# A hybrid attention, retention and ConvFFN layer on one core: loads of the merge in the order of use, a ring of its own for gate weights, and down-weight sums moved into the retention

## The chip, the core and the metric

The kernel runs on 1 core of one Trainium2 chip. The metric is device time in microseconds (us), the median of three runs. Matrix work runs on TensorE (PE; PEld is its weight load), elementwise work on VectorE (DVE), ScalarE (ACT) and GpSimd (POOL). All large transfers are issued from one queue, that of SyncE (SP). An instruction of an engine, and an issue of SP, starts only when the one before it on that engine has started or ended, so one that waits holds up whatever stands behind it.

## The reference, cut to what matters

One layer over 1024 latent tokens of width 1024 and 256 context tokens:

```python
hx = _modulate(_rmsnorm(x, norm1_g[l]), sh1, sc1)
(xq, xk, xv, xrq, xrk, xrv, xrg, xga, xgb) = jnp.split(hx @ w_in[l], IN_OFFSETS, axis=-1)
o_na = _na_latent(...)                 # 8 heads, neighbourhood attention plus context keys
o_ret = _ret_output(o_ret_x, xrg)      # 4 heads, both directions; normalized, times silu(xrg)
merged = sigmoid(xga) * (o_na @ w_proj_na) + sigmoid(xgb) * (o_ret @ w_proj_ret)
x = x + g1 * (merged @ w_out[l])
hx2 = _modulate(_rmsnorm(x, norm2_g[l]), sh2, sc2)
x = x + g2 * _conv_ffn(hx2, w_up[l], conv_w[l], conv_b[l], w_down[l])
return _rmsnorm(x, final_norm_g)
```

Everything is float32. Each operand of a large product is split into a high part (rounded to the type fp32r) and the remainder, and a product is made of three matmuls: high by high, high by low, low by high.

## The kernel before

The kernel is one Python function that writes out the layer stage by stage; a tile framework puts the instructions of a stage on the five queues, chooses their order within an engine from the dependences, and gives each tile a slot in a ring (`tag`, `bufs`). A tile waits until the slot's previous user is done. The stages, by time in the profile:

- Start and neighbourhood attention, up to 394 us. Filler work in it computes part of the gates ("spilled" ones, stored to DRAM as `d_gate`).
- Retention, 394 to 728 us: 4 heads (class `Head`), each over 2 context chunks and 8 latent chunks, so 40 steps, each called by `slot`. In a step `front` multiplies a chunk by the head's eight weight blocks, POOL adds the two parts of the rotation (tile `r`, L1115) and subtracts for `SS` (L1165), and `state` and the `mix` of the head before follow.
- NA projection, 728 to 788 us (L1313 to L1338): eight transposes groups `tpn` of the attention output read from DRAM, then for each of 8 blocks `db` two chains of 12 matmuls, `pn`. In between `hx_sums` builds eight sums of the input halves, `hxT`, on POOL, DVE and ACT.
- Gates, 795 to 953 us: 8 units (class `Gates`), each a Strassen-like scheme of 7 products (`Seven.step`) in place of 8; each product is 4 blocks by 3 matmuls. So 8 x 7 x 12 = 672 matmuls of 128x128 by 512. A unit loads four weight blocks `wr` (`Seven.load`) and POOL makes four sums of them. Units 0 to 3 produce the retention's output (stored as `d_orr`), units 4 to 7 the remaining merge gates.
- In the same stage, `down_sums` (11 rounds of 4, one every fifth product) loads four blocks `pj` of the down weights, subtracts on POOL (L1422, 44 in all) and stores them as `d_w`, for use at the end of the kernel.
- Merge, 953 to 1084 us: 16 blocks `orr` of the retention output are loaded and split, 32 blocks `sg` of gates and projections are loaded, the row vector `gate1` is loaded, and then for each of 8 `db` the two weight blocks of `w_pret` are loaded and split and two chains of 24 matmuls, `pr`, run: 384 matmuls.
- Output projection, 1084 to 1184 us (`out_proj`, products `om`; `w_out` is multiplied by `gate1` on POOL as it is loaded, L100), then the norm, the up products and convolution to 1640 us, and the down products to the end.

Weights pass through the helper `wload`: a load into the ring `raw` (3 tiles, L90), a copy on ACT to the high part (L86), a subtraction on DVE to the low part (L87), into a tile `wc` of a ring of 6. `orr` is loaded through the same three `raw` tiles.

Of the kernel before, what the change touches and what calls it, by code (L numbers as in the profile page):

```python
# [40 lines left out]
def tile_hybrid_layer(ctx, tc: tile.TileContext, io, dbg=None):  # L41
# [55 lines left out]
    def wload(src, lo_eng=None, mul=None, into=None):  # L97
        raw = rawload(src)
        if mul is not None:
            pool.tensor_tensor(raw, raw, mul, ALU.mult)  # L100
        wc = into if into is not None else wtile()
        split(wc[:, 0], wc[:, 1], raw, lo_eng)
        return wc
# [1121 lines left out]

    def slot(main, mix, head=None, i=None):
# [15 lines left out]
        if head:  # L1242
            head.state(i)
        if mix:
            mix.n += 1
# [30 lines left out]
    for _ in tl:  # L1276
        pass
# [5 lines left out]
    hcpool.release()  # L1283
    tg = sb("hx_sums", "right")
# [4 lines left out]
    NH = NF // 2  # L1289

    def g_ps(name):
        return pg.tile([P, 512], F32, tag="g", bufs=6, name=name)

# [5 lines left out]
    def hx_sums(k):  # L1299
        b = {}  # L1300
        for i, half in ((0, 1), (0, 0), (1, 1), (1, 0)):
            kb, c0 = k + KH * i, half * 512
            b[i, half] = t = onap.tile([P, 512], F32, tag="b", bufs=8, name="b")
# [9 lines left out]
    for n in range(KB):  # L1313
        raw = rawload(d_onat[n * P : (n + 1) * P])
# [6 lines left out]
    hs = None  # L1321
    for db in range(KB):
        wp = [wload(io["w_pna"][db, 0])]
        hs = hs if db % 2 else hx_sums(db // 2)
        for half in range(2):
            sl_ = slice(half * 512, half * 512 + 512)
            m = g_ps("pn")
            mm_a(m, wp, lambda k: ona[0][:, k, sl_], lambda k: ona[1][:, k, sl_])
            t = onap.tile([P, 512], F32, tag="pn", bufs=3, name="pn")
            if (db, 0) in spilled:  # L1330
                g = onap.tile([P, 512], F32, tag="sg", bufs=2, name="sgt")
                sync.dma_start(g, d_gate[2 * db, half])
                act.activation(g, g, AF.Sigmoid)
                vec.tensor_tensor(t, m, g, ALU.mult)
            else:
                act.copy(t, m)
            sync.dma_start(d_pn[db, half], t)
        next(hs)  # L1338
    pool.tensor_tensor(col[:, 16:48], col[:, 16:48], bcol[:, 16:48], ALU.add)  # L1339
    a2 = cpool.tile([P, KB], F32, name="a2")  # L1340
    pool.tensor_scalar(a2, col[:, 32:40], 1.0, None, ALU.add)
    pool.tensor_tensor(a2, a2, gcol[:, 1], ALU.mult)
    tpa = g_ps("tpa")
    pe.transpose(tpa[:32, :P], col[:, 16:48], ident)
    arow = ap_.tile([32, P], F32, name="arow")
    act.copy(arow, tpa[:32, :P])
    sync.dma_start(d_ada, arow)
    ap_.release()
    onap.release()


# [6 lines left out]
    class Seven:  # L1358
        def load(self):
            self.a21, self.a22, self.a11, self.a12 = [self.raw(self.src[b, i]) for b, i in ((1, 0), (1, 1), (0, 0), (0, 1))]  # L1360
# [16 lines left out]
        def step(self, n):  # L1377
            if n == 0:
                self.load()
# [28 lines left out]

    gr = sb("gates", "right")

    def down_sums():
        todo = []
        for j in range(NH):
            ts = []
            for i in range(2):
                for dh in range(2):
                    ts.append(gr.tile([P, 512], F32, tag="pj", bufs=8, name="pj"))
                    sync.dma_start(ts[-1], io["w_down"][dh, NH * i + j])
            while todo:
                sync.dma_start(*todo.pop())  # L1420
            for c, x, y, o in ((1, 1, 0, 0), (3, 3, 1, 1), (2, 3, 0, 3), (4, 2, 3, 2)):
                pool.tensor_tensor(ts[o], ts[x], ts[y], ALU.subtract)  # L1422
                todo.append((d_w[j, c - 1], ts[o]))
            yield
# [569 lines left out]
```

## Time and profile before

| what | us |
|---|---|
| median of 3 runs (1844.21 to 1849.22) | 1846.59 |
| the profiled execution | 1843.57 |
| its span, first to last instruction | 1841.4 |
| PE busy in the span | 1736.1 (94%) |
| DVE, ACT, POOL busy | 1314.1, 852.6, 604.0 |
| longest single idle time of PE | 42.6 |

The profile comes from one execution. A row of the waits names the engine that waited, what it wanted to do, and the instruction or transfer that ended the wait. A row of the timeline gives the start, the duration, and in brackets the idle time just ahead and its releaser. A table of windows gives the busy time of each engine in a stretch, and PEclk, the granted TensorE clock: 1.00 is 2.4 GHz, 0.50 is 1.2 GHz.

### The profile page before, as it was taken

The numbers are of one execution on the slowest core, as the hardware profiler recorded it, in microseconds if no ns is written. First come the engines' busy times: TensorE is split into PE (matmuls) and PEld (weight loads), VectorE is DVE, ScalarE is ACT, GpSimd is POOL, SyncE is SP. The second block draws the span as 40 slices with busy tenths as digits, with TensorE's granted clock in tenths as the row PEclk, the third lists the DMA queues.
The fourth block names the chain that finished last, engine by engine and source line by source line (L and its number), as shares of the span: only waits on it lengthen the run. The fifth ranks groups of instructions, "written<-read, shape, count | busy, mean of one in ns | idle before, by whom it ended". The sixth has DMA issues, their size and how long they took to land.

```text
span 1841.4 us, 24786 instructions
## 1 busy us (share of the span) xinstructions
PE 1736.1 (94%) x8381; PEld 1436.4 (78%) x8381; DVE 1314.1 (71%) x2450; ACT 852.6 (46%) x1841; POOL 604.0 (33%) x493
## 2 busy tenths in 40 slices
PE   8799999999999998989973999999999999999997
PEld 4588888888888887767853878878888888888886
DVE  5977887765676765767852465787999899885756
ACT  5666666653344443533332233454444444554444
POOL 2600000001323224277820350035555455311434
PEclk9899999999999999989996999999999999999999
DMA  9143334321010212568977243452332323486744
GB/s 350 48 120 127 103 123 136 111 83 41 18 58 18 58 58 79 167 233 304 342 243 248 58 131 137 176 199 86 115 115 89 111 86 115 147 292 192 238 154 173
DMA packets 139551, 261.61 MB, mean 142 GB/s; under 512 B 15872, under 2 KB 28320, under 8 KB 139424
## 3 DMA queue, kind: packets, MB, share of 16 engines
q1 hardware_dynamic: 139424, 260.03, 42.1%
q8 instruction: 66, 1.08, 0.3%
q14 instruction: 61, 0.50, 0.1%
HBM read 187.87 MB, written 69.48 MB: 140 GB/s over the span
## 4 chain that ended last, share of the span: by engine, by line
PE 71%; DVE 9%; issue 7%; DMA 6%; POOL 4%; ACT 3%; SPq 1%; POOLq 0%; ACTq 0%; DVEq 0%
PE u L1356 24%; PE y L1356 4%; PE mm L112 3%; PE mm L113 3%; PE mm L114 3%; PE mm L124 3%; PE mm L125 3%; PE mm L123 3%; PE R L511 2%; DVE wc L87 2%; PE ptp L493 2%; PE pr L112 1%; PE pr L113 1%; PE pr L114 1%; PE om L123 1%
## 5 line engine op out<-in xcount | busy, mean ns | idle before, releaser
L1356 PE MATMUL u<-T,wc 128*128 128x512 f32 x960 | 227.2, 392 | 4.1 <-ACT pu L1383 4.1
L1356 PEld LDWEIGHTS u<-T,wc 128*128 128x128 f32 x960 | 180.6, 189 | 45.2 <-ACT pu L1383 7.6
L1356 PE MATMUL y<-wc,ahl 128*128 128x512 f32 x924 | 210.6, 389 | 2.6 <-DVE wc L87 1.8
L1356 PEld LDWEIGHTS y<-wc,ahl 128*128 128x128 f32 x924 | 173.3, 188 | 39.6 <-DVE wc L87 2.5
L87 DVE TENSOR_TENSOR wc<-ur,wc 128x512 fp32r<-128x512 f32 x137 | 124.5, 911 | 65.4 <-ACT wc L86 65.4
L86 ACT CAST wc<-ur 128x512 fp32r<-128x512 f32 x137 | 85.1, 622 | 129.9 <-PE y L1356 72.3
L113 PE MATMUL mm<-low,wc 128*128 128x512 f32 (+1 forms) x328 | 124.0, 378 | 0.0
L1356 PE MATMUL u<-h2a,wc 128*128 128x512 f32 x480 | 112.4, 389 | 0.7 <-DVE pu L1391 0.7
L112 PE MATMUL mm<-hx,wc 128*128 128x512 f32 x264 | 107.2, 406 | 0.3 <-DVE vc L221 0.3
L1356 PEld LDWEIGHTS u<-h2a,wc 128*128 128x128 f32 x480 | 89.9, 188 | 19.9 <-DVE pu L1391 1.1
L114 PE MATMUL mm<-hx,wc 128*128 128x512 f32 x264 | 105.1, 398 | 0.0
L87 DVE TENSOR_TENSOR wc<-wr,wc 128x512 fp32r<-128x512 f32 x56 | 69.9, 1255 | 36.0 <-ACT wc L86 35.6
L1339 POOL TENSOR_TENSOR col<-col,bcol 128x32 f32<-128x32 f32 x1 | 0.3, 253 | 281.9 <-DVE aw L538 281.9
L1356 PE MATMUL u<-hxT,wc 128*128 128x512 f32 x384 | 90.4, 391 | 2.4 <-DVE pu L1391 2.4
L86 ACT CAST wc<-s 128x512 fp32r<-128x512 f32 x80 | 49.6, 622 | 91.9 <-PE u L1356 87.0
L125 PE MATMUL mm<-wc,low 128*128 128x512 f32 (+1 forms) x240 | 91.2, 380 | 0.0
L112 PE MATMUL pr<-orr,wc 128*128 128x512 f32 x128 | 50.7, 396 | 42.6 <-ACT wc L86 42.6
L87 DVE TENSOR_TENSOR wc<-raw,wc 128x512 fp32r<-128x512 f32 x92 | 70.5, 775 | 24.1 <-ACT wc L86 23.8
L87 DVE TENSOR_TENSOR wc<-s,wc 128x512 fp32r<-128x512 f32 x80 | 85.2, 1067 | 2.9 <-ACT wc L86 2.5
L1356 PEld LDWEIGHTS u<-hxT,wc 128*128 128x128 f32 x384 | 72.5, 189 | 17.9 <-issue 2.8
L86 ACT CAST wc<-raw 128x512 fp32r<-128x512 f32 x92 | 57.1, 622 | 43.6 <-DMA raw<-in_w_pret 16.1
L1362 POOL TENSOR_TENSOR s<-ur 128x512 f32<-128x512 f32 x20 | 36.9, 1844 | 121.0 <-DVE wc L87 70.5
(392 smaller groups left out, 4807.6 us busy)
## 6 DMA issues: line engine op xcount, KB each, us to landing
ur<-in_w_up SPq DMA_DIRECT2D x80, 256.0 KB, 2.8
ur<-d_a SPq DMA_DIRECT2D x77, 256.0 KB, 3.1
aw<-in_w_ada SPq DMA_DIRECT2D x32, 512.0 KB, 3.3
pj<-in_w_down SPq DMA_DIRECT2D x44, 256.0 KB, 5.2
d_w<-pj SPq DMA_DIRECT2D x44, 256.0 KB, 4.7
d_a<-sa SPq DMA_DIRECT2D x44, 256.0 KB, 2.0
ur<-d_w SPq DMA_DIRECT2D x44, 256.0 KB, 3.3
d_a<-at SPq DMA_DIRECT2D x33, 256.0 KB, 2.7
```

What stands on the lines that cost most here:

```text
L86: act.copy(hi, src)
L87: (lo_eng or vec).tensor_tensor(lo, src, hi.bitcast(F32), ALU.subtract)
L112: pe.matmul(out, wh, xh, start=k == 0, stop=False)
L113: pe.matmul(out, wh, xl, start=False, stop=False)
L114: pe.matmul(out, wl, xh, start=False, stop=k == n - 1)
L123: pe.matmul(out, ah, bh, start=first, stop=False)
L124: pe.matmul(out, ah, bl, start=False, stop=False)
L125: pe.matmul(out, al, bh, start=False, stop=last)
L493: pe.transpose(tp[:, c], self.Pm[h][:, c * P : (c + 1) * P], ident)
L511: pe.matmul(R[:, h], self.pair.V[:, g, h].rearrange("p a b -> p (a b)"), self.PT[h][:, c].rearrange("p a b -> p (a b)"), start=c == 0, sto ...
L1356: pe.matmul(out, a, b, start=first and n == 0, stop=last and n == 2, skip_group_check=True)
L1362: pool.tensor_tensor(self.s1, self.a21, self.a22, ALU.add)
```

## The change

Six edits:

1. `down_sums` is called from `slot` in the retention: two subtractions after each context step, one after each latent step, what is left after the last head. Its ring `pj` moves to the retention's pool. The subtractions keep their order on POOL.
2. A pool of its own (`rr`, ring `r` of 10 tiles) replaces three rings: it holds the attention output to be transposed, the tiles `b` of `hx_sums`, and the `wr` weights of the gates. It is allocated ahead of the NA projection and released after the gates. The transposed blocks no longer pass through `raw`.
3. The first gate unit's `load` is called at the end of the NA projection, not in the unit's first step.
4. In the merge, the loads come in the order of use: the first `w_pret` blocks, then for half 0 eight `orr` blocks and one `db` of `sg`, then the same for half 1, and from there one `db` of `sg` per step.
5. `w_out` is no longer multiplied by `gate1` on POOL (16 instructions); instead `out_proj` multiplies each product by `gate1` on DVE and then adds `x` (16 instructions more on DVE).
6. The classes stand ahead of the NA projection in the code.

```diff
+    def down_sums():
+        def load(j):
+            ts = [rt.tile([P, 512], F32, tag="pj", bufs=8, name="pj") for _ in range(4)]
+            for t, (i, dh) in zip(ts, ((0, 0), (0, 1), (1, 0), (1, 1))):
+                sync.dma_start(t, io["w_down"][dh, NH * i + j])
+            return ts
+
+        todo, nxt = [], load(0)
+        for j in range(NH):
+            ts, nxt = nxt, load(j + 1) if j + 1 < NH else None
+            for c, x, y, o in ((1, 1, 0, 0), (3, 3, 1, 1), (2, 3, 0, 3), (4, 2, 3, 2)):
+                late(pool.tensor_tensor(ts[o], ts[x], ts[y], ALU.subtract))
+                while todo:
+                    sync.dma_start(*todo.pop())
+                todo.append((d_w[j, c - 1], ts[o]))
+                yield
+        sync.dma_start(*todo.pop())
...
         if head:
             head.state(i)
+            for _ in range(2 if i < NCB else 1):
+                next(down_sums, None)
...
+    rr = sb("gate_raws", "right")
...
+    def g_raw(name):
+        return rr.tile([P, 512], F32, tag="r", bufs=10, name=name)
...
-            b[i, half] = t = onap.tile([P, 512], F32, tag="b", bufs=8, name="b")
+            b[i, half] = t = g_raw("b")
...
-        raw = rawload(d_onat[n * P : (n + 1) * P])
+        raw = g_raw("onr")
+        sync.dma_start(raw, d_onat[n * P : (n + 1) * P])
...
             if n == 0:
-                self.load()
+                if not self.loaded:
+                    self.load()
...
-            t = gr.tile([P, 512], F32, tag="r", bufs=10, name="wr")
+            t = g_raw("wr")
...
         next(hs)
+    gu[0].load()
...
-        if n % 5 == 2:
-            next(down_sums, None)
...
-    for half in range(2):
-        for db in range(KB):
-            split(*orr[half, db], rawload(d_orr[db, :, half * 512 : half * 512 + 512]))
     sg = {}
-    for db in range(KB):
+
+    def merge_load(db):
         for half in range(2):
             sg[db, 0, half] = gtile(half, F32, "sg")
             sync.dma_start(sg[db, 0, half], d_pn[db, half])
...
+    def orr_load(half):
+        for k in range(2 * RH):
+            split(*orr[half, k], rawload(d_orr[k, :, half * 512 : half * 512 + 512]))
...
         wp = [wload(io["w_pret"][db, i]) for i in range(2)]
+        if db + 1 < KB and db:
+            merge_load(db + 1)
         for half in range(2):
+            if db == 0:
+                orr_load(half)
+                merge_load(half)
             m = g_ps("pr")
             mm_a(m, wp, lambda k: orr[half, k][0], lambda k: orr[half, k][1])
...
-        wo[kb, 0] = wload(io["w_out"][0, kb], mul=gate1[:, 0:512], into=t)
+        wo[kb, 0] = wload(io["w_out"][0, kb], into=t)
...
-            vec.tensor_tensor(x1[:, cs], m, x1[:, cs], ALU.add)
+            vec.tensor_tensor(xr[:, cs], m, gate1[:, cs], ALU.mult)
+            vec.tensor_tensor(x1[:, cs], xr[:, cs], x1[:, cs], ALU.add)
```

What this does to the queues, in the words of the two programs (a row is one instruction or a run of equal ones; `out<-in`):

On SP before, at the end of the merge's loads, ahead of the first `pr` product (the 16 `orr` loads and 30 more `sg` loads stand ahead of these rows):

```order
L1502 DMA sg<-d_pn 128x512
L1504 DMA sg<-d_gate 128x512
L1511 DMA gate_10432<-d_ada 128x1024
L91 DMA raw<-in_w_pret 128x512 x16
L91 DMA raw<-in_w_out 128x512 x16
```

The weights of the products come after all loads of `orr` and `sg`.

On SP after, from the last gate units' stores on (`d_gate<-c` is the last one):

```order
L1451 DMA d_gate<-c 128x512
L1509 DMA sg<-d_pn 128x512
L1511 DMA sg<-d_gate 128x512
L1509 DMA sg<-d_pn 128x512
L91 DMA raw<-d_orr 128x512
L1451 DMA d_pn<-c 128x512
L91 DMA raw<-d_orr 128x512 x2
L1511 DMA sg<-d_gate 128x512
L1523 DMA gate_10300<-d_ada 128x1024
L91 DMA raw<-d_orr 128x512 x6
L1509 DMA sg<-d_pn 128x512
L91 DMA raw<-d_orr 128x512 x3
```

The two `w_pret` blocks of the first `db` and the first three `orr` blocks stand further up, among the gates. Thirteen `orr` loads are left behind the gates, with six `sg` loads and `gate1` between them, and `w_pret` for the second `db` follows them.

On SP before, between the NA projection and the gates:

```order
L1337 DMA d_pn<-pn 128x512 x10
L1347 DMA d_ada<-arow 32x128
L1442 DMA wr<-in_w_rg 128x512 x4
L1418 DMA pj<-in_w_down 128x512 x4
L1470 DMA o<-d_oret 128x512
L1442 DMA wr<-in_w_rg 128x512 x4
```

and after:

```order
L1421 DMA wr<-in_w_rg 128x512
L1471 DMA d_pn<-pnt 128x512
L1421 DMA wr<-in_w_rg 128x512 x3
L1471 DMA d_pn<-pnt 128x512 x4
L1421 DMA wr<-in_w_rg 128x512
L1471 DMA d_pn<-pnt 128x512 x2
L1482 DMA d_ada<-arow 32x128
L1421 DMA wr<-in_w_rg 128x512
```

The loads of the first two units moved up among the projection's stores.

On POOL in two steps of the retention, before:

```order
L1165 TENSOR_TENSOR SS<-run,SS 128x256
L1192 TENSOR_TENSOR mvr<-mvr,mhalf 128x1
L1115 TENSOR_TENSOR r_5631<-r_5631,r_5632 128x256
L1165 TENSOR_TENSOR SS<-init_4449,SS 128x256
L1165 TENSOR_TENSOR SS<-run,SS 128x256
```

and after:

```order
L1163 TENSOR_TENSOR SS<-run,SS 128x256
L1190 TENSOR_TENSOR mvr<-mvr,mhalf 128x1
L1113 TENSOR_TENSOR r_6376<-r_6376,r_6377 128x256
L1238 TENSOR_TENSOR pj<-pj 128x512
L1163 TENSOR_TENSOR SS<-st,SS 128x256
L1163 TENSOR_TENSOR SS<-run,SS 128x256
```

One subtraction of down weights now stands in each step between the rotation and `SS`.

## Rows read from the trace of the kernel before

**Rows 1.** Waits of PE, 730 to 1240 us: total, times, longest.

```profile
PE pr L112 <- ACT wc L86: 42.6, 1, 42.6
PE u L1356 <- ACT wc L86: 7.0, 1, 7.0
PE om L123 <- ACT mh L86: 4.5, 1, 4.5
...
PE tpn L1317 <- DMA raw<-d_ona: 3.3, 4, 1.2
PE u L1356 <- DVE pu L1391: 2.4, 1, 2.4
PE pn L112 <- ACT wc L86: 1.7, 1, 1.7
```

**Rows 2.** Timeline of PE: start, duration, instruction, idle before and releaser.

```profile
740.59 0.80 PE L112 MATMUL pn<-ona,wc 128*128 128x512 f32 x1 [1.70 <-ACT wc L86]
...
794.61 0.79 PE L1356 MATMUL u<-hx,wc 128*128 128x512 f32 x1 [7.04 <-ACT wc L86]
...
952.85 0.39 PE L1356 MATMUL u<-hx,wc 128*128 128x512 f32 x1
995.88 0.79 PE L112 MATMUL pr<-orr,wc 128*128 128x512 f32 x1 [42.64 <-ACT wc L86]
...
1003.03 0.39 PE L112 MATMUL pr<-orr,wc 128*128 128x512 f32 x1
...
1008.47 0.39 PE L112 MATMUL pr<-orr,wc 128*128 128x512 f32 x1
```

**Rows 3.** Windows of stages: length, busy (instructions) PE PEld DVE ACT POOL, PEclk, DMA share, GB/s.

```profile
394.00:650.00 256.00, 254.66 (x1346) 217.79 (x1346) 167.90 (x564) 105.19 (x304) 63.38 (x92) 1.00 0.13 40
...
728.00:789.00 61.00, 53.15 (x227) 42.52 (x227) 41.00 (x57) 28.84 (x52) 21.95 (x16) 0.92 0.51 160
...
800.00:955.00 155.00, 150.86 (x662) 124.22 (x660) 116.33 (x118) 55.49 (x97) 112.24 (x72) 1.00 0.83 286
...
1083.00:1195.00 112.00, 107.54 (x492) 88.43 (x492) 69.85 (x174) 40.15 (x86) 10.39 (x13) 0.98 0.43 153
```

**Rows 4.** Windows just after PE resumed, columns as in rows 3.

```profile
794.60:797.00 2.40, 2.27 (x5) 1.36 (x6) 2.27 (x2) 1.14 (x2) 2.40 (x3) 0.50 1.03 379
...
996.00:999.00 3.00, 3.00 (x7) 2.31 (x8) 1.80 (x3) 1.07 (x2) 0.00 (x0) 0.50 0.47 128
```

**Rows 5.** Timeline of SP's issues from the end of the gates.

```profile
954.59 0.32 SPq L91 DMA_DIRECT2D raw<-d_orr  x1
...
974.98 0.32 SPq L91 DMA_DIRECT2D raw<-d_orr  x1
...
989.20 51.10 SPq L91 DMA_DIRECT2D raw<-in_w_pret  x16
```

**Rows 6.** DMA issues, 950 to 1000 us: count, KB each, median us to landing.

```profile
raw<-d_orr SPq DMA_DIRECT2D x13, 256.0 KB, 4.0
```

**Rows 7.** Landing of the 32 loads into `raw`, 394 to 730 us.

```profile
DMA to landing us min/median/max: 2.5/2.7/4.3
```

**Rows 8.** Groups by form in the gates, 800 to 955 us: busy, mean ns.

```profile
L1422 POOL TENSOR_TENSOR pj<-pj 128x512 f32<-128x512 f32 x44 | 69.9, 1589 | 8.1 <-DMA pj<-in_w_down 2.6 <-issue 2.3 <-DMA d_w<-pj 1.1
L87 DVE TENSOR_TENSOR wc<-wr,wc 128x512 fp32r<-128x512 f32 x53 | 65.4, 1239 | 17.8 <-ACT wc L86 17.5
...
L86 ACT CAST wc<-wr 128x512 fp32r<-128x512 f32 x52 | 30.6, 617 | 32.4 <-POOL wr L1363 10.3 <-DMA wr<-in_w_rg 9.8 <-PE u L1356 7.2
...
L1374 DVE TENSOR_TENSOR c<-u,pu 128x512 f32<-128x512 f32 x24 | 16.3, 680 | 8.8 <-PE u L1356 8.7
```

**Rows 9.** Timeline of POOL at the end of the merge.

```profile
1082.30 1.29 POOL L100 TENSOR_TENSOR raw<-raw,gate 128x512 f32<-128x512 f32 x1 [1.84 <-DMA raw<-in_w_out]
```

**Rows 10.** Timeline of DVE where a head's last weight block is split.

```profile
534.16 0.68 DVE L87 TENSOR_TENSOR wx<-raw,wx 128x512 fp32r<-128x512 f32 x1
```

**Rows 11.** Timeline of PE at the first use of that block's low part.

```profile
535.18 0.34 PE L125 MATMUL mm<-wx,low 128*128 128x384 f32 x1
```

More of the change, by code (lines that the diff above doesn't have):

```diff
@@ L1275, in tile_hybrid_layer @@
         slot(pieces3(tl), mix)
-    for _ in tl:
-        pass
+    for it in (tl, down_sums):
+        for _ in it:
+            pass
     prt.release()
@@ L1406, in interleaved @@
         return [(i, k) for _, i, k in sorted((7 * i + 2 * k, i, k) for i in range(n0, n) for k in range(7))]
[L1409 to L1424, printed above, removed]
-        while todo:
-            sync.dma_start(*todo.pop())
-    down_sums = down_sums()
     class Gates(Seven):
@@ L1475, in tile_hybrid_layer @@
     gu = [Gates("ret", h) for h in range(RH)] + [Gates("merge", db) for db in range(nsp, KB)]
-    for n, (i, k) in enumerate(interleaved(0, len(gu))):
+    hs = None
+    for db in range(KB):
+        wp = [wload(io["w_pna"][db, 0])]
+        hs = hs if db % 2 else hx_sums(db // 2)
+        for half in range(2):
+            sl_ = slice(half * 512, half * 512 + 512)
+            m = g_ps("pn")
+            mm_a(m, wp, lambda k: ona[0][:, k, sl_], lambda k: ona[1][:, k, sl_])
+            t = onap.tile([P, 512], F32, tag="pn", bufs=3, name="pnt")
+            if (db, 0) in spilled:
+                g = onap.tile([P, 512], F32, tag="sg", bufs=2, name="sgt")
+                sync.dma_start(g, d_gate[2 * db, half])
+                act.activation(g, g, AF.Sigmoid)
+                vec.tensor_tensor(t, m, g, ALU.mult)
+            else:
+                act.copy(t, m)
+            sync.dma_start(d_pn[db, half], t)
+        next(hs)
+    gu[0].load()
+    pool.tensor_tensor(col[:, 16:48], col[:, 16:48], bcol[:, 16:48], ALU.add)
+    a2 = cpool.tile([P, KB], F32, name="a2")
+    pool.tensor_scalar(a2, col[:, 32:40], 1.0, None, ALU.add)
+    pool.tensor_tensor(a2, a2, gcol[:, 1], ALU.mult)
+    tpa = g_ps("tpa")
+    pe.transpose(tpa[:32, :P], col[:, 16:48], ident)
+    arow = ap_.tile([32, P], F32, name="arow")
+    act.copy(arow, tpa[:32, :P])
+    sync.dma_start(d_ada, arow)
+    ap_.release()
+    onap.release()
+    gr = sb("gates", "right")
+    for i, k in interleaved(0, len(gu)):
         gu[i].step(k)
-        if n % 5 == 2:
-            next(down_sums, None)
-    for _ in down_sums:
-        pass
     gr.release()
     tg.release()
+    rr.release()
     hxpool.release()
```

42 lines of the change are left out of this document (7 added, 35 removed).

## The prediction, made before the changed kernel ran

> **What bounds the kernel now.** I read the page's shares first: PE is busy 1736.1 of 1841.4 us, so the kernel can only gain where PE idles or runs at its lower clock, and it loses where the change makes PE wait. So the next view is the list of PE's waits in the stages that the diff touches [rows 1]: one of 42.6 us before the first merge product `pr`, one of 7.0 before the gates, one of 4.5 in the output projection, and 3.3 and 1.7 in the NA projection. Then the timeline of PE around each [rows 2] gives the length of each stage, and the windows show the clock [rows 4]: at 0.50 (1.2 GHz) just after the gates' start and after the merge's, both behind idle time; the middle of the gates runs at 1.00 [rows 3]. In the merge 24 matmuls take 1008.47 − 1003.03 = 5.44 us [rows 2], 0.2267 us each. That is PE's price at full clock. Last, in the retention PE is busy 254.66 of 256 us and POOL 63.38, and in the gates POOL is busy 112.24 of 155 [rows 3]: the change takes POOL work from a stage where it is dense to one where PE has nothing to lose.
>
> **NA projection (edit 2).** The `tpn` transposes wait 3.3 us in four pieces for blocks that go through three `raw` slots, and the first `pn` waits 1.7 us for the first split weights, which share these slots [rows 1]. With ten slots of their own for the blocks, and the first weights loaded and split in the tail of the retention, both waits should go: 5.0. Clock: `pn` starts at 740.59 and ends at 794.61 − 7.04 = 787.57 [rows 2]. That is 46.98 us for 8 x 2 x 12 = 192 matmuls, which at 0.2267 take 43.5; so 3.4 are lost, mostly to the low clock (the window's mean is 0.92 [rows 3]). I take 2.0 of it, because the idle time of the retention's last head ahead of `tpn` stays and PE may still start low. Gain **7.0**; bounds 4.0 (0.6 of the waits lost to loads that now come in one burst, and 0.4 to the clock) and 8.4. The loads hoisted into that stretch find the DMA half idle (share 0.51 [rows 3]).
>
> **Gates' start and gates (edits 1 to 3).** The 7.04 us wait on the first split `wr` [rows 1]; POOL must first have finished `hx_sums`, since its order is that of the code. After the change, the loads of units 0 and 1 stand among the stores of `pn`, and POOL's sums behind the last `hx_sums`. The whole `pn` chain of the last blocks covers them; if it does not, the 7.0 stays. Then the gates themselves: from 794.61 to 995.88 − 42.64 = 953.24 [rows 2] are 158.63 us; 8 x 7 x 12 = 672 matmuls at 0.2267 take 152.3. Of the 6.3 over, 2.4 is a wait on DVE [rows 1] and 3.9 is what the low clock at the start leaves [rows 4]. If PE goes from `pn` into the gates without idling, 7.0 and 3.9 go, and of the 2.4 I take half, because DVE becomes faster in places: 44 subtractions of 1589 ns leave POOL [rows 8]. Gain 7.0 + 3.9 + 1.2 = **12.1**; bounds 6.0 (the wait halved, 3.5, with 2.5 of the clock) and 13.3.
>
> **Merge (edit 4).** Before, from the end of the gates to the first matmul of `db` 1 it is 1008.47 − 953.24 = 55.2 us: the 42.64 wait and 48 matmuls, partly slow. The queue shows why: SP issues 16 `orr` loads through three slots, 13 of them from 954.59 to 974.98 [rows 5], and only at 989.20 the first `w_pret` [rows 5]. So twelve intervals take 20.39 us, **1.70** each. It is the ring that paces them: 4.0 us to land [rows 6] and a good 1.1 for the split make 5.1 for three slots, 1.70 each. In the retention the same ring's loads land in 2.7 (median) [rows 7]; then a load costs (2.7 + 1.1) / 3 = 1.27. After the change 13 `orr` loads are still left behind the gates, but `w_pret` of `db` 0 is in, and only 6 of the `sg` loads and `gate1` stand among them. Between 1.27 and 1.70 I take 1.5, the middle: less traffic than before, but in the same slots. The first issue is 1.35 after the gates' end (954.59 − 953.24), 13 more intervals bring `w_pret` of `db` 1: 1.35 + 13 x 1.5 + 4.0 + 1.3 for its cast (0.62) and subtraction (0.68) [rows 8, 10] = 26.2. The 48 matmuls of `db` 0 (10.9 us) lie inside. The new pauses will let the clock fall again, as all idle stretches of this length did [rows 4]: before, the first 24 `pr` matmuls took 1003.03 − 995.88 = 7.15 where 5.44 is full clock [rows 2], 1.7 lost; I take 2. Gain 55.2 − 26.2 − 2 = **27.0**. Bounds: at 1.27 and a landing of 2.7 the time is 1.35 + 16.5 + 2.7 + 1.3 = 21.9, gain 32 (with 1 for the clock); at 1.70, with a slot's turn of 2.2 lost to `sg`, it is 31, gain 22.
>
> **Output projection (edit 5).** The 4.5 us wait of `om` [rows 1] is for the last split merge tile, and POOL's part in it stands behind the multiplications by `gate1`: one waits 1.84 for its block of `w_out` and then takes 1.29 [rows 9], and the last merge additions stand behind it on POOL. Without the 16 multiplications these additions start at once: gain **4.4**; bounds 0 (the last load of `sg` takes their place) and 4.5. The price is 16 DVE instructions in `out_proj`. Their form isn't in the trace; the nearest is DVE's 680 ns with one operand from PSUM [rows 8], so 16 x 0.68 = 10.9 us on DVE, which is busy 69.85 of 112 there [rows 3] and stays under PE. PE meets it only where the last token block's norm is awaited, two of these instructions: cost **1.0**, bounds 0 and 3 (the accumulator bank is also held 0.7 longer per product).
>
> **Retention (edit 1).** This is where the change pays. 44 subtractions of 1.59 us come in [rows 8], 70 us on POOL in 334, which leaves it under half busy if the share of 63.38 in 256 [rows 3] holds for the whole. Each stands between the rotation and `SS` in its step, so `SS` is late by 1.6 us where its down weights have landed, and by more where not; a step is 8.3 us of PE work (334 / 40), and `SS` serves the next one. SP gets 44 loads and 44 stores in the same steps, and a store waits on POOL with the head's weights queued behind it. These are the tight ones: a head's last block ends its split at 534.16 + 0.68 = 534.84 [rows 10] and its first matmul starts at 535.18 [rows 11], 0.34 later. So at three head boundaries PE will wait for whatever SP is late; one POOL instruction (1.6) less the 0.34 is 1.2 for each, 3.7 in all: cost **4.0**. Bounds: 0 (the loads go out earlier, because the scheduler sees slots free), and 14 (the whole landing time of 4.3 [rows 7] plus 0.3 at each of three boundaries).
>
> DVE's subtraction took 1239 ns with POOL busy 112.24 of 155 [rows 8, 3], and the same form 0.68 in the retention [rows 10]. The Trainium skill, page "SBUF — State Buffer", section "Who interferes with whom", says that a DVE instruction with two SBUF inputs and a GpSimd instruction that reads SBUF exclude each other, the second being fully blocked. The rows agree. By that rule the edit would give the gates' DVE time back and take it from the retention: at worst 44 times 1.59 us on top of DVE's 66% there, which would leave DVE at 87%, an estimate that changes the sum only if such a block falls on the chain from PE to PE within a step; it speaks against the edit, and with every block on that chain the time would be rival 1's.
>
> **The sum.** 7.0 + 12.1 + 27.0 + 4.4 − 1.0 − 4.0 = 45.5, against the profiled execution's 1843.6: 1798.1. The median of the runs is 1846.59, 3.0 above that execution; I add it: **1801**. All bounds together on one side give 1788 (58.2 gained) and 1832 (15 gained); the half-widths 2.2, 3.7, 5, 2.2, 7 and 1.5 as independent errors make 10, so the likeliest case's own range is 1789 to 1815.
>
> **Rivals.**
> 1. *The retention pays in full (slower).* The steps of the retention have no slack: POOL's subtraction, DVE blocked beside it, or SP's queue lies on the chain of each step, and all 44 x 1.59 = 70 us reach PE. The other parts bring 49.5, so the kernel would be 20.4 slower: 1867. It turns at 49.5 / 40 = 1.24 us lost per step. For it: POOL's instruction stands ahead of `SS` in every step. Against it: 8.3 us of a step with POOL busy two of them, and PE's products of the head before that need no `SS`. Chance 0.04, and as much again for a half-way loss of about 45 us, which ends within 0.3%.
> 2. *The merge's wait only moves into `db` 0.* The six `sg` loads and `gate1` count in the pace as much as `orr` does: 20 x 1.70 + 1.35 + 5.3 = 40.7 in place of 26.2, a gain of 12.5: 1801 + 14.5 = 1816. For it: DMA's share is high at the end of the gates (0.83 [rows 3]), and the slots stay three. Against it: `sg` has slots of its own and needs no split. Chance 0.14.
> 3. *The gates still wait for their first weights* (the ten slots are shared with `hx_sums`, whose slots come free late, so the loads can't start): 7.0 and 3.9 stay, 1812. Chance 0.09.
> 4. *Everything is covered:* the merge runs at 1.27 per load, the clock stays up and the retention loses nothing: 1788. Chance 0.10.
>
> **How the numbers follow.** The forecast has 0.59, and the rivals 0.08, 0.14, 0.09 and 0.10 as told. The range reaches from 1784 (rival 4 with 4 us of room) to 1823 (rival 2 with half its own error of 14); what lies outside is rival 1, its half-way form, and the tails of rivals 2 and 3 together, below 0.2. A difference of 0.3% (5.5 us) is about what a measurement of this kernel can tell from none. Rivals 2 to 4 and the forecast are all faster than that, even with all bad bounds at once (1832): faster 0.92; the half-way loss gives same 0.04, rival 1 slower 0.04.
>
> **What would show it.** In the profile after: PE's 42.6 wait gone, and in its place several of 1 to 4 us in `db` 0 that end with the cast or subtraction of an `orr` block; `db` 1 starting 24 to 31 us after the gates' end (over 36: rival 2). No wait above 2 us ahead of the gates, and 154 to 157 us from their first matmul to their last (rival 3 otherwise). No `om` wait above 1 us. The retention's PE time up by about 4 us, with waits on `raw` loads at the first matmul of heads 1 to 3; waits of PE in every step on `SS` or DVE would be rival 1. DVE's subtraction of `wc` in the gates nearer to 700 than to 1239 ns. I would be most wrong if SP, which waits in order, held the retention's weights behind a store that waits on POOL by more than one instruction.

## The result and the profile after

The changed kernel takes 1817.99 us (median of 4 runs, 1815.95 to 1819.02) beside 1846.04 before (1844.21 to 1849.22): a ratio of 0.9845, 95% interval 0.9828 to 0.9862. It gains 28 us where 45 were forecast; the time lies inside the range, near its upper end. The profiled span went from 1841.4 to 1814.2. In stretches cut at the first instructions of the stages, in us:

| stretch | before | after | gain | forecast |
|---|---|---|---|---|
| start to first `tpn` (attention, retention) | 729.6 | 750.6 | −21.0 | −4.0 |
| first `tpn` to first gate matmul | 65.0 | 50.5 | 14.5 | 14.0 |
| gates | 158.6 | 152.4 | 6.2 | 5.1 |
| end of gates to first `om` | 131.4 | 107.5 | 23.9 | 27.0 |
| first `om` to first `u` on `T` | 148.6 | 142.1 | 6.5 | 3.4 |
| up products and convolution | 378.1 | 381.1 | −3.0 | 0 |
| down products to the end | 230.1 | 230.0 | 0.1 | 0 |

Four stretches gain about what was said, 51.1 against 49.5. The retention costs five times its price. The waits of PE behind the retention in the changed kernel, of the same view as [rows 1] (total, times, longest):

```profile
PE pr L110 <- ACT orr L86: 7.6, 6, 2.1
PE u L1353 <- ACT pu L1384: 5.0, 1, 5.0
...
PE pr L111 <- DVE orr L87: 2.3, 6, 1.2
PE tpn L1345 <- DMA onr<-d_ona: 1.0, 1, 1.0
```

The waits of 42.6, 7.0 and 4.5 us of [rows 1] are gone; `pr` now waits in twelve small pieces, and of the NA projection's five us one is left. The windows, with the columns of [rows 3], of the retention, the gates and `db` 0 of the merge:

```profile
394.00:745.00 351.00, 339.10 (x1731) 285.27 (x1729) 238.74 (x710) 137.93 (x396) 146.62 (x170) 0.98 0.35 111
...
801.00:951.00 150.00, 150.00 (x663) 124.23 (x662) 83.85 (x116) 58.65 (x97) 35.60 (x26) 1.00 0.44 147
955.00:977.00 22.00, 15.28 (x38) 8.62 (x38) 9.83 (x15) 9.02 (x16) 1.73 (x1) 0.77 0.66 235
```

In the gates PE is busy without a break at full clock, beside a POOL with 35.6 us of work where [rows 3] had 112.2. The retention is the reverse: PE is idle for 12 of 351 us, and its clock, 1.00 before [rows 3], is 0.98 on average. So time is lost there in two ways, in waits and in stretches at 1.2 GHz. DVE's split in the gates, as in [rows 8]:

```profile
L87 DVE TENSOR_TENSOR wc<-wr,wc 128x512 fp32r<-128x512 f32 x52 | 36.2, 696 | 24.4 <-ACT wc L86 24.0
```

The same subtraction took 1239 ns while POOL was dense [rows 8], and takes 696 now.

**Where the retention's 21 us lie.** Setting the matmuls of `dS` of the two traces side by side, step by step, most steps have the length they had. The three boundaries between heads (around the last latent step of one head and the first two steps of the next) cost 4.4, 5.6 and 6.2 us, and two latent steps of each of heads 1 to 3 cost 0.67 each, 4.0 in all; the context steps of the first head cost the last 0.9. The first boundary on DVE and POOL after, two timelines (start, duration, instruction, idle before):

```profile
455.12 2.87 DVE L87 TENSOR_TENSOR wc<-raw,wc 128x512 fp32r<-128x512 f32 x2
457.91 1.77 DVE L87 TENSOR_TENSOR wx<-raw,wx 128x512 fp32r<-128x512 f32 x1
```

```profile
454.99 0.73 POOL L1113 TENSOR_TENSOR r<-r,r 128x256 f32<-128x256 f32 x1 [6.03 <-DVE r L1112]
455.68 3.44 POOL L1238 TENSOR_TENSOR pj<-pj 128x512 f32<-128x512 f32 x2
459.09 1.19 POOL L1163 TENSOR_TENSOR SS<-st,SS 128x256 fp32r<-128x256 f32 x1
```

And PE there, then the clock, in windows with the columns of [rows 3]:

```profile
458.04 0.44 PE L122 MATMUL mm<-wc,hc 128*128 128x384 f32 x1 [0.62 <-DVE wc L87]
459.73 0.44 PE L122 MATMUL mm<-wx,hc 128*128 128x384 f32 x1 [0.72 <-DVE wx L87]
```

```profile
456.00:458.00 2.00, 1.42 (x9) 1.02 (x7) 2.00 (x3) 1.88 (x6) 1.92 (x2) 1.00 0.00 1
...
462.00:464.00 2.00, 2.00 (x8) 1.90 (x8) 1.81 (x4) 0.57 (x2) 0.00 (x0) 0.50 0.82 287
```

Beside POOL's rotation and two down-weight subtractions (3.44 us), DVE's three splits of the head's weights take 1.15, 1.79 and 1.77 us, where the split of [rows 10] took 0.68. The ends of the single instructions (the rows above merge equal neighbours) show more: the rotation ends at 455.72, the subtractions at 457.44 and 459.13, and the splits at 456.27, 457.99 and 459.68, each 0.55 later. In the whole retention all 14 splits of over 1 us end 0.55 us (0.545 to 0.550) after an instruction of POOL has ended, and the nine subtractions of over 1.5 us end 1.14 to 1.17 after one of DVE. So the two engines take turns, a whole instruction at a time, and the duration of one contains its wait for the other. PE, which needs each block right after its split, waits, and then runs some us at half clock.

In the two latent steps it is the same with a smaller instruction: DVE's `kz`, which reads `r` and `kz` from SBUF, stands behind a subtraction (the 80 of the retention take 622 ns in the mean, before 382), the tile `A` is late behind it, and a transpose on PE waits 0.44 us.

That suggests a cause, but POOL's subtraction, the transfers and the instructions' order all changed at once.

### The profile page after: what moved, and what is told of

Same layout as the page of the kernel before. It is cut to its first block, busy times and chain, and to the rows that moved or that the text cites. A ratio compares the mean times of both kernels' runs of the same rounds, so it can differ in the third digit from the quotient of the medians.

```text
span 1814.2 us, 24862 instructions
## 1 busy us (share of the span) xinstructions
PE 1750.3 (96%) x8381; PEld 1442.3 (80%) x8381; DVE 1304.7 (72%) x2466; ACT 853.5 (47%) x1841; POOL 563.6 (31%) x477
## 4 chain that ended last, share of the span: by engine, by line
PE 67%; DVE 10%; issue 9%; POOL 6%; DMA 5%; ACT 3%; SPq 1%; POOLq 0%; ACTq 0%; DVEq 0%
PE u L1353 27%; PE y L1353 4%; PE mm L110 3%; PE mm L112 3%; PE mm L111 3%; PE R L509 2%; PE mm L122 2%; PE mm L123 2%; PE mm L121 2%; PE ptp L491 2%; PE pr L110 2%; PE pr L111 2%; PE pr L112 1%; PE om L122 1%; PE om L121 1%
## 5 line engine op out<-in xcount | busy, mean ns | idle before, releaser
L121 PE MATMUL mm<-wc,hx 128*128 128x512 f32 x192 | 75.3, 392 | 0.6 <-ACT r L1103 0.6
L122 PE MATMUL mm<-wc,hx 128*128 128x512 f32 x192 | 75.3, 392 | 0.0
```

The lines of the kernel that those rows point to most:

```text
L121: pe.matmul(out, ah, bh, start=first, stop=False)
L122: pe.matmul(out, ah, bl, start=False, stop=False)
```

## The experiments

In these, "the dS stretch" is the time from the first to the last high-by-high matmul of `dS`: 282.9 us before (399.7 to 682.6), 304.1 after (399.3 to 703.4). The expectations take neighbouring matmuls as its ends, so that their figures differ by some tenths. The stretch repeats well: in the changed kernel and in three below that keep edit 1 whole (those on the merge's ring and on edits 5 and 3) it is 303.4 to 304.1 us, so that a single run tells a difference of 2 us in it.

**Edit 1 undone.** `down_sums` and its call every fifth product are back in the gates; all other edits stay.

```diff
-            for _ in range(2 if i < NCB else 1):
-                next(down_sums, None)
...
+    for n, (i, k) in enumerate(interleaved(0, len(gu))):
         gu[i].step(k)
+        if n % 5 == 2:
+            next(down_sums, None)
```

> The changed kernel with edit 1 undone: the 44 subtractions of down weights and their 88 transfers stand in the gates again, all other edits stay. In the changed kernel the retention, taken from the first to the last matmul of dS, lasts 303.8 us (399.3 to 703.1), before 282.6 (399.7 to 682.3). Theory: all of these 21 us come from edit 1, so the stretch goes back to 283 +-1. In the gates POOL is dense again; if the gates' 6 us gain came from the undisturbed start alone they stay at 152 to 154 us and the kernel takes about 1797 us; if it needs POOL's absence (DVE's subtractions slow again, sums of weights late) the gates go back to 156 to 158 and the kernel takes about 1802. Rival: the 21 us come from something else that moved in the retention (hoisted loads, the order of PE's instructions); then the stretch stays at 300 or more.

1804.64 us; ratio to before 0.9772 (0.9752 to 0.9792). So **without edit 1 the change gains 42 us in place of 28**; the intervals of the two ratios don't meet. The dS stretch is that of before:

```profile
L121 PE MATMUL dS<-v,kz x80: 277/282/386, 395.6 to 678.5; 128*128 128x256 f32 x80
```

The gates need POOL's absence even more than was thought: they last 161.5 us, longer than before and than the expectation's 156 to 158, with these waits and groups:

```profile
PE u L1330 <- DVE pu L1364: 3.7, 1, 3.7
PE u L1330 <- ACT wc L86: 1.4, 1, 1.4
```

```profile
L1477 POOL TENSOR_TENSOR pj<-pj 128x512 f32<-128x512 f32 x42 | 67.3, 1606 | 5.7 <-DMA d_w<-pj 2.8 <-issue 0.6
...
L87 DVE TENSOR_TENSOR wc<-wr,wc 128x512 fp32r<-128x512 f32 x46 | 57.3, 1248 | 23.5 <-ACT wc L86 23.1
```

So edit 1 gives 9 us in the gates and takes 21 in the retention.

**The transfers without the subtractions.** The 88 transfers stay in the retention, and the subtractions are left out.

```diff
-                late(pool.tensor_tensor(ts[o], ts[x], ts[y], ALU.subtract))
```

> The changed kernel without the 44 POOL subtractions (left out: what is stored as down sums are the loaded blocks themselves); the 44 loads and 44 stores of edit 1 stay in the retention, at the same places on the queue. Theory A (POOL: its subtractions lie beside DVE's splits of a head's weights and ahead of work that PE waits for): the stretch from first to last dS matmul falls from 303.8 to 283 to 286 us. Theory B (the queue and the DMA: stores and loads of down weights hold the head's weight blocks back): it stays at 298 to 304.

1794.2 us (one run). The dS stretch is 291.3 us: neither theory's figure. But of the 8.4 us over before, 7.8 lie at the first boundary and nearly all of the rest in the step behind it; the other two boundaries cost nothing. PE at the first, and windows of the DMA (share is the last column but one):

```profile
453.68 0.69 PE L121 MATMUL mm<-wc,hc 128*128 128x384 f32 x1 [5.30 <-ACT wc L86]
```

```profile
445.00:450.00 5.00, 3.37 (x20) 2.87 (x18) 0.42 (x1) 0.08 (x1) 0.00 (x0) 1.00 0.90 276
450.00:455.00 5.00, 1.28 (x3) 0.89 (x4) 1.34 (x5) 1.81 (x4) 0.00 (x0) 0.73 0.93 296
```

With no subtraction to wait for, the loads and stores run ahead: all 88 are issued by 480 us, where in the changed kernel the last ones go out at 680, and the DMA's share is 0.90 just where the second head's weights are loaded. So transfers can hold a head up when they bunch. At the second and third boundary no transfers of down weights are left, so this run doesn't show what they cost there; the last run below has all 88 spread over the retention.

**The subtractions without the transfers.** Down sums in the gates, and 44 subtractions on two resident tiles at the places of edit 1 (the lines that make the tiles are left out here).

```diff
+            for _ in range(2 if i < NCB else 1):
+                if len(done_) < 44:
+                    done_.append(1)
+                    late(pool.tensor_tensor(idle[0], idle[0], idle[1], ALU.subtract))
```

> Down sums back in the gates as in the run sums_in_gates, and in the retention, at the places of edit 1 (two per context step, one per latent step), 44 subtractions of the same size on POOL on two tiles that are always there: no transfers. Theory A (POOL): the stretch from first to last dS matmul is 297 to 304 us, with DVE's weight splits at the start of a head at 1.2 to 1.5 us each in place of 0.69. Theory B (queue and DMA): 283 to 286 us, whatever DVE's splits take.

1822.6 us (one run), 18 more than with the sums in the gates alone. The orders of instructions on PE and DVE are the same in both, word for word. The dS stretch is 302.4 us, so 19.5 us, nearly all of the 21, come without any transfer and without a change of PE's order. Theory A holds.

**Writing only.** The same (the edit is against the run before), but the 44 instructions are memsets of 128x1280, which read nothing.

```diff
-                    late(pool.tensor_tensor(idle[0], idle[0], idle[1], ALU.subtract))
+                    late(pool.memset(idle[0], 0.0))
```

> As the run pool_only (down sums in the gates, 44 extra instructions on POOL at the places of edit 1, no transfers), but the extra instruction only writes: a memset of 128x1280, whose length by the rows of pool_only (532 ns for 128x512) is about 1.33 us, that of its subtraction there 1.29. It takes POOL's time in the same way and reads nothing. Theory C (while POOL reads two operands, DVE's instructions with two operands in SBUF stand still): DVE's splits of wx go from 1226 ns back to about 690, and the three head boundaries, 9.5 us in pool_only, fall to under 3. Theory D (POOL's own order: its extra instruction delays the rotation and SS behind it): the boundaries cost as much as in pool_only, with DVE's splits at 690 ns. Against sums_in_gates: C about +2 us, D about +10.

1797.73 us (one run). Groups of DVE's split and `kz` and of POOL's extra instruction in the retention (busy, mean ns), and waits of PE, first with the subtraction, then with the memset (two of the 44 memsets lie outside the window):

```profile
L87 DVE TENSOR_TENSOR wx<-raw,wx 128x512 fp32r<-128x512 f32 x6 | 7.4, 1226 | 0.0
L1132 DVE SCALAR_TENSOR_TENSOR kz<-r,dec,kz 128x128 fp32r<-128x128 f32 x80 | 52.3, 685 | 22.1 <-ACT kz L1131 21.8
...
L1254 POOL TENSOR_TENSOR idle<-idle,idle 128x512 f32<-128x512 f32 x44 | 61.4, 1394 | 1.2
```

```profile
PE dS L123 <- DVE kz L1132: 2.7, 5, 0.7
PE tpo L1197 <- DVE A L1171: 2.6, 6, 0.4
PE mm L122 <- DVE wc L87: 2.2, 3, 0.8
PE mm L122 <- DVE wx L87: 1.9, 3, 0.8
PE tp L1121 <- POOL r L1113: 1.2, 2, 0.8
```

```profile
L87 DVE TENSOR_TENSOR wx<-raw,wx 128x512 fp32r<-128x512 f32 x6 | 4.1, 691 | 0.3
L1132 DVE SCALAR_TENSOR_TENSOR kz<-r,dec,kz 128x128 fp32r<-128x128 f32 x76 | 27.1, 371 | 25.1 <-ACT kz L1131 24.9
...
L1252 POOL MEMSET idle<- 128x1280 f32 x42 | 49.1, 1169 | 0.5
```

```profile
PE mm L121 <- ACT r L1103: 0.6, 1, 0.6
PE mm L122 <- DVE wx L87: 0.6, 2, 0.3
```

The dS stretch is 282.4 us: **nothing is lost.** PE, DVE and ACT have the same instructions in the same order in both runs. POOL's memsets are somewhat shorter (1.17 us for 1.39) and not all in the same places: 39 of the 44 stand between the same two instructions, five stand behind one `SS` more, so that `SS` at the first boundary is held up by 0.1 us where the subtractions held it up by 4.3. The rows tell that this is not what makes the difference: with the subtractions, 9.4 us of PE's waits are on DVE's `kz`, `A` and splits, and none on `SS`; and in the latent steps of heads 1 to 3, where the places are the same, the 1.3 us per head are gone with the memsets too. So this pair of runs settles the cause: what costs is not POOL's time but that POOL reads from SBUF while DVE runs instructions with two operands there. That is the rule that the prediction had from the Trainium skill, page "SBUF — State Buffer", section "Who interferes with whom"; the rows agree with its further point that a GpSimd instruction which only writes does not contend with such an instruction of DVE. That DVE's two operands matter shows in the gates of the run with edit 1 undone: 18 instructions of DVE that take one operand from PSUM (`c<-u,pu`, `pu<-u,pu`) began while POOL subtracted and took 0.67 to 0.69 us, like the 680 ns of [rows 8], where splits that began so took up to 1.78. (Whether one operand read by POOL would do was not tried.) The whole time is 7 us below that of the run with edit 1 undone, where about 2 more were expected; this comes from stretches that the memsets don't touch (up products 3.4, down products 2.8, merge 2.1, gates 2), in one profile each, and nothing here rests on it.

**Other steps for the subtractions.** None in the context steps, with twelve moved to the end of the retention:

```diff
-            for _ in range(2 if i < NCB else 1):
+            if i >= NCB:
                 next(down_sums, None)
...
         slot(pieces3(tl), mix)
+        for _ in range(2):
+            next(down_sums, None)
```

> The changed kernel with the subtractions of edit 1 (and so their transfers) taken out of the context steps, where a head's weights are loaded and split: one after each latent step, and the 12 that are left two at a time in the last steps of the retention, where only the mix of the last head runs. The three head boundaries cost 16 of the 21 us in the changed kernel, and two latent steps per head 0.67 each. Both theories A and B expect the boundaries' cost to go: the stretch from first to last dS matmul 286 to 290 us, the kernel about 1803 to 1806 us. A rival (any subtraction costs its share wherever it stands) expects 298 or more and 1815.

1810.23 us, ratio 0.9801 (0.9775 to 0.9827); the dS stretch is 298.0, so the expectation failed: each boundary still costs 3.2 to 3.9 us, and 4.8 more come at the stretch's end, where the first of the twelve stand. POOL's timeline shows why: at each boundary two subtractions, those of the last latent steps, stand in the same place as in the changed kernel, behind the last rotation. The first:

```profile
457.22 3.44 POOL L1238 TENSOR_TENSOR pj<-pj 128x512 f32<-128x512 f32 x2
```

Then only in latent steps 1 to 6 (`if 2 <= i <= 7`), twenty at the end:

> The changed kernel with the subtractions of edit 1 only where no weights of a head are split and no context step is near: one in each of latent steps 1 to 6 of a head (24), the other 20 two at a time in the last ten steps of the retention. In none_in_context two of them still stood on POOL at each head boundary, since POOL's order had let the one of the last latent step fall behind the next head's rotation. Theory C/A: the stretch from first to last dS matmul is 283 to 287 us (before 283.2, changed 304.4), the rest of the kernel as in the changed one, so about 1800 us. Rival (the transfers of edit 1 on the shared queue cost by themselves): 290 or more, about 1806.

1813.93 us, ratio 0.9823 (0.9800 to 0.9846). The dS stretch falls to 290.8, the rival's figure; DVE's `wx` splits are back at 686 ns, but 1.5 to 2.2 us remain at each boundary and 2 come at the stretch's end. The longest of PE's waits in it are now on POOL's rotation (3.3 us in four). Transfers still come in at the boundaries, and PE's order there differs from that of before; these runs do not separate the two. And the twenty subtractions at the end bring a wait of their own, since the attention output's blocks stand behind their transfers on the queue:

```profile
750.91 4.50 PE L1347 MATMUL tpn<-ident,onr 128*128 128x128 f32 x20 [5.90 <-DMA onr<-d_ona]
```

**The merge's ring.** The 13 `orr` loads behind the gates go to the tiles that `w_out` fills later, two to a tile, in place of the three `raw` slots.

```diff
-            split(*orr[half, k], rawload(d_orr[k, :, half * 512 : half * 512 + 512]))
+            src = d_orr[k, :, half * 512 : half * 512 + 512]
+            if half == 0 and k < 3:
+                raw = rawload(src)
+            else:
+                if not pair:
+                    t = wop.tile([P, 2, 512], F32R, tag="wo", bufs=KB, name="orw")
+                    pair.extend((t[:, 0].bitcast(F32), t[:, 1].bitcast(F32)))
+                raw = pair.pop()
+                sync.dma_start(raw, src)
+            split(*orr[half, k], raw)
```

> The changed kernel, with the 13 orr loads that stand behind the gates put into slots of their own (the tiles that w_out fills later), in place of the three raw slots. Theory: what paced the merge at 1.78 us per load (955.02 to 976.33 for twelve intervals) is the ring of three, landing 4 us plus split; with free slots the loads go out at SP's pace and the DMA's rate is the bound: 13 blocks and 7 other loads of 256 KB at 300 to 350 GB/s are 15 to 17 us, so db 1 starts 18 to 22 us after the gates' end in place of 29.8; the kernel gains 8 to 11 us, about 1808. Rival: the DMA's rate or the splits on ACT and DVE set the pace already; then db 1 starts after 27 to 30 us as now, 1816 to 1818.

1809.71 us, ratio 0.9801 (0.9775 to 0.9826). SP issues the 13 loads in 9.9 us, and the DMA is then full:

```profile
959.46 9.86 SPq L1525 DMA_DIRECT2D orw<-d_orr  x13
```

```profile
953.00:975.00 22.00, 12.19 (x41) 8.30 (x39) 12.01 (x18) 12.21 (x21) 1.33 (x1) 0.77 0.98 347
```

From the first `pr` to the first `om` it is 101.0 us in place of 107.5, and `db` 1 begins 24.7 us after the gates, in place of 29.8 and of the expected 18 to 22. So the ring of three did set the pace; without it the DMA does, with a share of 0.98 at 347 GB/s.

**Edit 5 undone** (`gate1` multiplied into `w_out` on POOL as before, one instruction fewer per product in `out_proj`):

```diff
-        wo[kb, 0] = wload(io["w_out"][0, kb], into=t)
+        wo[kb, 0] = wload(io["w_out"][0, kb], mul=gate1[:, 0:512], into=t)
...
-            vec.tensor_tensor(xr[:, cs], m, gate1[:, cs], ALU.mult)
-            vec.tensor_tensor(x1[:, cs], xr[:, cs], x1[:, cs], ALU.add)
+            vec.tensor_tensor(x1[:, cs], m, x1[:, cs], ALU.add)
```

> The changed kernel with edit 5 undone: gate1 multiplied into w_out on POOL. Theory: the merge's last additions stand behind these multiplications again, so om waits about 4.5 us and PE's clock falls, and the stretch from first pr to last om, 200.2 us in the changed kernel, becomes 205 to 208; the kernel takes about 1823. Rival: with the merge's loads in the new order the blocks of w_out are there in time, nothing is held up, and the wait does not come back: 1816 to 1819. Beside it: the first wait in the up products is 5.0 us in the changed kernel, 3.75 before; if the added DVE work of edit 5 is the reason it goes back to 3.75.

1818.39 us, ratio 0.9851 (0.9828 to 0.9874): by the times no difference can be told. By the profile the stretch from the first `pr` to the last `om` is 204.1 us, just below the theory's 205; the products `om` take 97.0 us from first to last in place of 92.7, with the wait about half as long as in [rows 1]:

```profile
PE om L123 <- ACT mh L86: 2.4, 1, 2.4
```

So in the profile edit 5 is worth 2.4 us of wait and 1.9 more, which lower clock behind the wait would explain, once the merge's loads come in the new order. The wait in the up products stays, and so is not edit 5's.

**Edit 3 undone** (no early call of the first unit's load):

```diff
-    gu[0].load()
```

> The changed kernel with edit 3 undone: the first gate unit's loads and sums are called in its first step again; its own ring (edit 2) stays. If the early call is what takes away the 7.0 us wait before the gates, a wait of 3 to 7 us comes back there and the clock falls behind it (gates 154 to 157 in place of 152.6). Rival: the ring is enough, since its slots are free and the loads move up by themselves; then no wait above 1 us and the gates stay at 152.6.

1815.7 us (one run). No wait before the gates, which last 152.6 us as in the changed kernel. The ring of edit 2 is enough.

**The subtractions on DVE.** If POOL's reading is the cause, the same subtractions on DVE should be cheap, in either place. First in the gates, with the merge's ring (`vec.tensor_tensor` for `pool.tensor_tensor`):

> Down sums in the gates as in sums_in_gates, but subtracted by DVE in place of POOL, and the orr loads in slots of their own as in merge_ring. Theory C (what costs in the gates and in the retention is POOL reading beside DVE's two-operand instructions): with POOL idle for most of the gates DVE's splits of wr are at about 700 ns in place of 1248, the added 44 x 0.7 = 31 us on DVE go beside 79 of 139, and the gates last 152.5 to 155 us in place of 161.5; the retention is as before the change (283). The kernel: 1804.6 of sums_in_gates, less 7 for the gates, less 7 for the merge: about 1791. Rival (the gates are long because of the 88 transfers of down weights there, or because any engine's subtraction holds others up): gates at 158 or more, 1796 to 1798.

1796.68 us, ratio 0.9712 (0.9695 to 0.9729). The gates last 158.2 us, 3 less than with POOL, but 6 more than without the subtractions: the rival's figure. DVE's splits take 867 ns, and its queue waits:

```profile
L1477 DVE TENSOR_TENSOR pj<-pj 128x512 f32<-128x512 f32 x44 | 32.6, 740 | 18.3 <-DMA pj<-in_w_down 14.8 <-issue 3.1
```

The subtraction itself is short, but DVE stands 14.8 us for its blocks to land, with the splits queued behind it. That suggests that in the gates part of the price is the transfers', whose landing DVE awaits in order; the run doesn't separate this from the rival's other reason, that any engine's subtraction holds the splits up.

Then in the retention, at the places of edit 1, with the merge's ring:

```diff
-                late(pool.tensor_tensor(ts[o], ts[x], ts[y], ALU.subtract))
+                late(vec.tensor_tensor(ts[o], ts[x], ts[y], ALU.subtract))
```

> The changed kernel with the 44 subtractions at the same places of the retention, but on DVE in place of POOL (about 0.7 us each in place of 1.6), and the orr loads in slots of their own as in merge_ring. Theory C: no instruction of POOL holds DVE up any more, so of the 21 us in the retention only what DVE's own 31 us cost at the head boundaries stays, 3 to 8 us; gates 152.6, merge 7 less: about 1796 to 1800. Rival (transfers and the order of the instructions cost most of the 21 us): the retention stays 15 to 21 us longer than before, 1806 to 1811.

**1791.88 us**, ratio 0.9689 (0.9673 to 0.9705), faster than both kernels: 26 us below the changed one, of which merge_ring had 8 by itself. The dS stretch and all waits of PE in the retention:

```profile
L121 PE MATMUL dS<-v,kz x80: 277/282/388, 401.8 to 686.2; 128*128 128x256 f32 x80
```

```profile
PE dS L121 <- ACT kz L1131: 1.2, 3, 0.4
PE mm L121 <- ACT wx L86: 0.9, 3, 0.3
PE mm L121 <- ACT r L1103: 0.6, 1, 0.6
```

The stretch is 284.4 us, 1.5 over before, less than either expectation, with all 44 subtractions and 88 transfers in it. So at these places the transfers cost next to nothing. And moving the down sums into the retention was a gain after all, about 5 us against the same subtractions on DVE in the gates (1791.88 to 1796.68; no run of the one is as slow as the fastest of the other); the engine was the wrong one.

## Why the prediction was right or wrong

One row of before is needed beside [rows 10, 11], PE's timeline again:

```profile
534.90 0.44 PE L124 MATMUL mm<-wx,hc 128*128 128x384 f32 x1
```

It is the first matmul that reads what DVE's split in [rows 10] writes, the block's low part. The split ends at 534.84. The matmul of [rows 11], 0.28 us later, takes the block's high part and the low part of the chunk.

- **NA projection** (7.0): right. The stretch and the gates' start gained 14.5 where 14.0 were said; less the 7.0 wait this is 7.5. Its two parts were each off by about 1, in opposite directions: the waits gave 4 where 5.0 were said, and the clock some 3 where 2.0 were said (`pn` lasts 43.8 us where it lasted 47.0). That the sum fits is partly luck.
- **Gates** (12.1): right in size, 7.0 + 6.2 = 13.2, just below the upper bound of 13.3. That DVE's subtraction would come near 700 ns is borne out (696). Wrong in its cause for the start as far as edit 3 goes: without the early call nothing changes, so edit 2's ring is enough. No run takes edit 2 back. And the sum hid how much edit 1 carries here: with POOL's subtractions back, the gates last 161.5, so 9 us hang on their absence.
- **Merge** (27.0): the mechanism was right and the size 3 us too good, at the pace per load. I took 1.5 us between 1.27 and 1.70; the twelve intervals took 21.3 us (955.02 to 976.33), 1.78 each, a little above the pace of before [rows 5] and outside the two ends that I set. The rows of the retention [rows 7] were the wrong neighbour, since there the DMA is nearly idle (13% in [rows 3]) and here it is at 0.66; the 13 loads took 3.9 us to land (median), about the 4.0 of before [rows 6]. Rival 2, that the wait would only move into `db` 0, did not come: `db` 1 begins 29.8 us after the gates, not 40.7.
- **Output projection** (4.4 − 1.0): 6.5. Beside the 4.5 of the wait some 2 come from the products themselves, which I had left out: the clock no longer falls behind that wait. The 16 DVE instructions (688 ns each) cost PE no wait.
- **Retention** (−4.0): **this is the step that failed.** The place was right, the head boundaries. The price was not. I priced one POOL instruction of delay on the queue, 1.2 us per boundary, with landing time as the upper bound; measured were 4.4 to 6.2 per boundary, 4.0 in latent steps and 0.9 in the first head, 21 in all, beyond the bound of 14. What was left out is that DVE itself is held up: it takes turns with POOL, its splits last 1.15 to 1.79 us in place of 0.69, one behind the other, and then the clock is lower after the waits. The rule that says so stood in the prediction, and the sentence that it changes the sum only if the block falls on the chain from PE to PE was true. The row that shows that it does fall there was misread. The matmul of [rows 11] takes the block's high part and the chunk's low part; the first that reads what DVE's split writes is the one ahead of it (the row above), 0.06 us after the split's end and not 0.34. So there was next to no slack to set against a longer split. Rival 1 had the right mechanism, but not for every step: of its 70 us, 21 came true, since most latent steps have slack.
- **Up products** (0): −3.0, not foreseen. Their first long wait, on ACT, is 5.0 us in the changed kernel and was 3.75 before, which is 1.25 of the 3.0; in the other runs it is between 4.0 and 6.4. Undoing edit 1 or edit 5 does not bring it back. What sets it stays open.

The total, 28, is thus not the forecast's sum with a small error in each term but the forecast's gains with one term wrong by 17; the other stretches are off by 3 us or less each. The time stayed inside the range, although the retention left its own bounds, because the other parts brought what was said.

## What to carry to other kernels

Before work is moved to an idle GpSimd, look not at its idle time but at what VectorE does beside it: if VectorE runs instructions there that read two operands from SBUF and that PE awaits within a fraction of a us, a GpSimd instruction that reads from SBUF can hold them up, here by up to 1.1 us each, and short waits can then cost clock as well. Before a margin is read off two rows, look up which operand the later one reads. In a stage where VectorE has room, giving it the instruction (0.7 to 0.9 us here) can be far cheaper than giving it to GpSimd (1.3 to 1.7 us). And when a price is bounded by neighbouring rows, take rows with the same load on the DMA.

## What the runs showed of the hardware

- 44 POOL subtractions of 128x512, 1.39 us each and all operands resident, lengthened a stretch of 283 us by 19.5; 44 POOL memsets, 1.17 us each, 39 of them at the same places, by nothing.
- POOL's subtraction and DVE's instructions with two operands in SBUF took turns: a split held up by POOL ended 0.55 us after POOL's instruction, a `kz` 0.15 us after it. POOL's subtraction took 1.29 us in the median and up to 1.76 in the retention, 1.61 in the mean among DVE's splits in the gates; DVE's split 0.69 alone, 1.25 in the gates, up to 1.79 at a boundary.
- TensorE's clock was at its lower level (0.50, 1.2 GHz) from 462 to 464 us behind three waits of 0.56, 0.62 and 0.72 us, so that short waits cost more than their sum: of the 21 us in the retention the waits of PE's list make up about 11, and by an estimate from the mean clock (0.98 in place of 1.00 over the 311 us from 394 to 705) some 6 are the clock's.
- The first 394 us, which no edit touches, differ by some us from profile to profile: the first `dS` matmul starts between 395.2 and 402.7 us. That is a reason to compare stages and not spans.
